# Recording the HGRN2 recurrence beside the next preparation, and stick-breaking attention as one pipeline over all query tiles

## The chip, the cores and the metric

The program runs on all 8 cores of one Trainium2 chip (two dies of four cores), two of the sixteen sequences on each core, the same program on every core. The metric is the device time in microseconds (us) of the slowest core. Such a program has two states: in some executions the cores of one die, or of both, show a lower granted TensorE clock and take some per cent longer. A run is called slow when one die is over 1% longer than the other at a lower clock, or when it is over 1.5% above the fastest run of the same kernel.

Engine names in the profile: PE is TensorE (PEld its weight loads), DVE is VectorE, ACT is ScalarE, POOL is GpSimd.

## The reference

Two layers of an encoder. Each layer is half a feed-forward step, a mixer with three branches (latent attention A, stick-breaking attention B, the gated recurrence HGRN2 C), a gated merge, another half feed-forward step and an added input embedding. The change touches branches B and C only:

```python
def stick_breaking_attention(q, k, v):            # 8 heads of 64, per block of queries
    z = einsum('bqhd,bkhd->bhqk', q, k) * scale
    mask = pos_k < pos_q
    log_beta = log_sigmoid(z)
    log_keep = where(mask, log_sigmoid(-z), 0.0)
    log_rest = cumsum(log_keep, reverse=True) - log_keep        # over the keys
    a = where(mask, exp(minimum(log_beta + log_rest, 0.0)), 0.0)
    return einsum('bhqk,bkhd->bqhd', a, v)

def hgrn2_recurrence(q_raw, f_raw, i_in, g_raw, lb, norm_w):    # 4 heads, chunks of 64
    ...                                                          # [cut: gates, cumulated logs]
    def step(state, xs):                                         # over the 32 chunks
        qd_n, kd_n, v_n, decay_n = xs
        o_n = einsum('bhck,bhkv->bhcv', qd_n, state)
        state = decay_n[..., None] * state + einsum('bhck,bhcv->bhkv', kd_n, v_n)
        return state, o_n
    ...                                                          # [cut: norm and output gate]
```

## The kernel before

The kernel records operations with the tiles that they read and write; a small layer turns these into semaphore waits, and each engine gets its operations in the order in which they were recorded. So the order of recording is the order of each engine's queue.

HGRN2, for each of the four heads: `prep` is a generator with 12 steps per tile of 512 tokens, and the four tiles take turns; then the recurrence runs alone.

```python
def prep(t, sl):
    mm(ps[b], [(whg[:, k, 128:256], uT[:, k, tok]) for k in range(8)])   # forget gate
    act(x1, ps[b], AF.Exp, scale=-1.0)
    yield
    mm(...); act(QF[:, tok], ps[b], AF.Silu); ts(x1, x1, 1.0, None, ALU.add)
    yield
    mm(...); act(GS[:, tok], ps[b], AF.Silu); reciprocal(x2, x1)          # VectorE
    yield
    ...          # [cut: V projection; Ln; scan; subtract; two Exp; three products; transposes]

interleave([prep(t0 + i, i) for i in range(min(NCHAIN, NT - t0))])        # four tiles
for t in range(NT):
    for j in range(4):
        mm1(ps[ba], KF[:, blk], QF[:, blk]); tt(Am, ps[ba], mhg_f, ALU.mult)   # mask product
        mm1(ps[bo], Vt[:, m, :], Am)
        for cch in range(2):                                              # two chunks
            mm1(ps[bo], Sbf[:, sl, :], QF[:, chunk])
            mm1(ps[bs_], KFt[pr, m, :], Vt[pr, m, :])
            stt(St, St, dec[:, c:c+1], ps[bs_], ALU.mult, ALU.add)
            ts(Sbf[:, 1 - sl, :], St, e1[:, c+1:c+2], None, ALU.mult)
    ...          # [cut: tail of a tile: Square, sum by matmul, Ln, Exp, two products]
```

Stick-breaking, for each of two groups of four heads: 16 query tiles (four heads, four tiles of 512), and for each a three-stage pipeline over blocks of 128 keys, which is emptied at the tile's end. A job is one block of keys. The first four jobs of a tile are its diagonal jobs, into whose blocks the mask cuts: they have 128, 256, 384 and 512 of the tile's queries. All later ones are full jobs of 512. In the comments below U is a triangle of ones, spb the masked logarithm and R its running sum over the keys already done.

```python
for hl in range(4):
    for tq in range(NT):
        for idx, kc in enumerate(range(nk - 1, -1, -1)):      # nk = 4, 8, 12, 16 jobs
            # stage 1: z = k.q ; Exp ; Ln(1 + .) ; mask ; R += (GpSimd and VectorE) ; Rb = bf16(R)
            # stage 2 of the job before: z again, + (-U).spb, + (-1).Rb, all into one bank ; Exp ; mask
            # stage 3 of the job before that: out += v.a
        ...      # [cut: the last two stages run out]
        cp(yB[...], ps[bo][0:64, :])                           # VectorE
```

The softmax here doesn't subtract the row's maximum and nothing guards it: scores larger than these inputs give would overflow.

Of the kernel before, what the change touches and what calls it, by code (L numbers as in the profile page):

```python
# [191 lines left out]
def build(nc, S, NSEQ, layers=(0, 1), phases=('ffa', 'mix', 'ffb', 'ple'), final_norm=True, dbg=None):  # L192
# [302 lines left out]
    def mixer(l, sq_i, branches):  # L495
# [152 lines left out]
        def branch_c():  # L648
# [29 lines left out]
            NCHAIN = min(4, NT)  # L678
# [7 lines left out]
            for h in range(4):  # L686
# [4 lines left out]
                def prep(t, sl):  # L691
# [6 lines left out]
                    b = bank()  # L698
# [3 lines left out]
                    b = bank()  # L702
# [4 lines left out]
                    b = bank()  # L707
# [4 lines left out]
                    b = bank()  # L712
# [31 lines left out]
                    b = bank()  # L744
# [10 lines left out]

                for t0 in range(0, NT, NCHAIN):
                    interleave([prep(t0 + i, i) for i in range(min(NCHAIN, NT - t0))])
                P.add('dve', lambda e: e.memset(St, 0.0), w=['St'])
                P.add('dve', lambda e: e.memset(Sbf[:, 0, :], 0.0), w=[('Sbf', 0)])
                ai = 0  # L760
                for t in range(NT):
                    tok = slice(t * 512, (t + 1) * 512)
                    bo = bank()
                    for j in range(4):
                        m = t * 4 + j
                        blk = slice(m * 128, (m + 1) * 128)
                        cols = slice(j * 128, (j + 1) * 128)
                        ba = bank_x(bo)
                        mm1(ps[ba][:, 0:128], KF[:, blk], QF[:, blk], True, True, r=[('KF', t), ('QF', t)], w=[PSK(ba)])
                        a_ = ai % 2  # L770
                        ai += 1
                        tt(Am[:, a_, :], ps[ba][:, 0:128], mhg_f, ALU.mult, r=[PSK(ba), 'cstf'], w=[('Am', a_)])
                        mm1(ps[bo][:, cols], Vt[:, m, :], Am[:, a_, :], True, False, r=[('Vt', t), ('Am', a_)], w=[PSK(bo)])
                        for cch in range(2):
                            c = 2 * m + cch
                            sl = c % 2
                            mm1(ps[bo][:, j * 128 + cch * 64:j * 128 + (cch + 1) * 64], Sbf[:, sl, :], QF[:, c * 64:(c + 1) * 64],
                                False, cch == 1, r=[('Sbf', sl), ('QF', t)], w=[PSK(bo)])
                            if c == NCH - 1:
                                continue  # L780
                            bs_ = bank_x(bo)
                            pr = slice(cch * 64, (cch + 1) * 64)
                            mm1(ps[bs_][:, 0:128], KFt[pr, m, :], Vt[pr, m, :], True, True, r=[('KFt', t), ('Vt', t)], w=[PSK(bs_)])
                            stt(St, St, dec[:, c:c + 1], ps[bs_][:, 0:128], ALU.mult, ALU.add, r=['St', PSK(bs_), ('dec', c // 8)], w=['St'])
                            ts(Sbf[:, 1 - sl, :], St, e1[:, c + 1:c + 2], None, ALU.mult, r=['St', ('e1', (c + 1) // 8)], w=[('Sbf', 1 - sl)])
                    sq = tmp['sq']
                    x1, x2 = X[0][0], X[0][1]
                    act(sq[:, 0, :], ps[bo][:, :], AF.Square, r=[PSK(bo)], w=[('sq', 0)])
                    bss = bank_x(bo)
                    mm1(ps[bss][:, :], ones_b, sq[:, 0, :], True, True, r=[('sq', 0), 'cstb'], w=[PSK(bss)])  # L790
                    act(x1, ps[bss][:, :], AF.Ln, r=[PSK(bss)], w=[('x', 0, 1)], scale=1.0 / 128, bias=epsc)
                    act(x1, x1, AF.Exp, r=[('x', 0, 1)], w=[('x', 0, 1)], scale=-0.5)
                    tt(x2, ps[bo][:, :], x1, ALU.mult, r=[PSK(bo), ('x', 0, 1)], w=[('x', 0, 2)])
                    stt(yC[:, h, tok], x2, nwcol(l, 37, h), GS[:, tok], ALU.mult, ALU.mult, r=[('x', 0, 2), ('GS', t), nwk], w=[('yT', 2)])
# [9 lines left out]
        def branch_b():  # L804
            for g in range(2):
# [35 lines left out]
                wi_ = 0  # L841
                for hl in range(4):
                    cc = hl // 2
                    pb = (hl % 2) * 64
                    hg = g * 4 + hl
                    for tq in range(NT):
                        qtok = slice(tq * 512, (tq + 1) * 512)
                        bo = bank()
                        nk = 4 * (tq + 1)
                        P.add('pool', lambda e: e.memset(R[:, 256:512], 0.0), w=[('R', 1)])  # L850
                        P.add('dve', lambda e: e.memset(R[:, 0:256], 0.0), w=[('R', 0)])
                        pend2 = None
                        pend3 = None
                        for idx, kc in enumerate(range(nk - 1, -1, -1)):
                            j = kc - 4 * tq
                            c0 = 128 * j if j > 0 else 0
                            cs = slice(c0, 512)
                            q = wi_ % 2
                            q3 = wi_ % 3
                            wi_ += 1  # L860
                            bz = bank_x(bo)
                            kap = kT[pb:pb + 64, cc, kc * 128:(kc + 1) * 128]
                            qap = qT[pb:pb + 64, cc, tq * 512 + c0:(tq + 1) * 512]
                            mm1(ps[bz][:, cs], kap, qap, True, True, r=[('kT', kc // 4), ('qT', tq)], w=[PSK(bz)])
                            act(e32[:, q, cs], ps[bz][:, cs], AF.Exp, r=[PSK(bz)], w=[('e32', q)])
                            act(spb[:, q3, cs], e32[:, q, cs], AF.Ln, r=[('e32', q)], w=[('spb', q3)], bias=onec)
                            if j >= 0:
                                tt(spb[:, q3, c0:c0 + 128], spb[:, q3, c0:c0 + 128], msb_b, ALU.mult, r=[('spb', q3), 'cstb'], w=[('spb', q3)])
                            if idx < nk - 1:
                                rs_ = idx % 4  # L870
                                jn = j - 1
                                c0n = 128 * jn if jn > 0 else 0
                                hi0 = max(c0, 256)
                                tt(R[:, hi0:512], R[:, hi0:512], spb[:, q3, hi0:512], ALU.add, r=[('R', 1), ('spb', q3)], w=[('R', 1)], eng='pool')
                                if c0 < 256:
                                    tt(R[:, c0:256], R[:, c0:256], spb[:, q3, c0:256], ALU.add, r=[('R', 0), ('spb', q3)], w=[('R', 0)])
                                cp(Rb[:, rs_, c0n:512], R[:, c0n:512], r=[('R', 0), ('R', 1)], w=[('Rb', rs_)])
                            p3 = pend3
                            pend3 = None
                            if pend2 is not None:  # L880
                                pend2()
                            if p3 is not None:
                                p3()

                            def stage3(idx=idx, kc=kc, cs=cs, q3=q3):
                                mm1(ps[bo][0:64, cs], vS[:, kc, hl * 64:(hl + 1) * 64], ab[:, q3, cs], idx == 0, idx == nk - 1,
                                    r=[('vS', kc // 4), ('ab', q3)], w=[PSK(bo)], skip=True)

                            def stage2(idx=idx, kc=kc, j=j, c0=c0, cs=cs, q3=q3, kap=kap, qap=qap, st3=stage3):
                                nonlocal pend3  # L890
                                bc = bank_x(bo)
                                rsl = (idx - 1) % 4

                                def fn(e):
                                    e.matmul(ps[bc][:, cs], kap, qap, start=True, stop=False)
                                    ins = e.matmul(ps[bc][:, cs], nuinc_b, spb[:, q3, cs], start=False, stop=(idx == 0))
                                    if idx > 0:
                                        ins = e.matmul(ps[bc][:, cs], nones_b, Rb[:, rsl, cs], start=False, stop=True)
                                    return ins
                                P.add('pe', fn, r=[('kT', kc // 4), ('qT', tq), ('spb', q3), 'cstb'] + ([('Rb', rsl)] if idx > 0 else []), w=[PSK(bc)])  # L900
                                act(ab[:, q3, cs], ps[bc][:, cs], AF.Exp, r=[PSK(bc)], w=[('ab', q3)])
                                if j >= 0:
                                    tt(ab[:, q3, c0:c0 + 128], ab[:, q3, c0:c0 + 128], msb_b, ALU.mult, r=[('ab', q3), 'cstb'], w=[('ab', q3)])
                                pend3 = st3
                            pend2 = stage2
                        if pend3 is not None:
                            p3 = pend3
                            pend3 = None
# [171 lines left out]
```

## Time and profile before

The six runs have a median of 14,892.7 us (14,829 to 15,087). The profiled run is a slow one.

I cut the trace at the first weight transfer of each stage (for the loops of B at the first clearing of the running sum R). The times are sums over four passes, mean of the eight cores:

| stage | us | mean TensorE clock, lowest to highest core |
|---|---|---|
| feed-forward, two halves | 4,123 | 0.92 to 0.97 |
| HGRN2 (C) | 1,940 | 0.62 to 0.63 |
| latent attention (A) | 1,987 | 0.82 to 0.84 |
| projections of B | 914 | 0.69 to 0.73 |
| the eight loops of B | 3,267 | 0.51 to 0.53 |
| merge and embedding | 2,464 | 0.90 to 0.95, 0.68 to 0.69 |

How to read the lines in this document: in a timeline a line is start, duration (us), engine, source line, operation, tiles, shapes; `x3` are three instructions that followed each other, and the bracket is the idle time of the engine before it and what ended it. `ps` are the banks that TensorE writes its sums to, `arena` the kernel's working memory, `cstb` and `cstf` constants such as the masks. In a table by stretch a line is the stretch and its length, then for each engine its busy time and number of instructions, then the granted TensorE clock and the DMA's share.

### The profile page before, as it was taken

What the parts mean: (1) busy time and instruction counts of PE and PEld (TensorE: products, weight loads), DVE (VectorE), ACT (ScalarE), POOL (GpSimd) and SP (SyncE); (2) the same over time, 40 slices, a digit from 0 to 9 for tenths busy, and PEclk for the clock granted to TensorE, in tenths of its full rate; (3) what the DMA queues carried; (4) which work ended last, traced back from release to release, by engine and by line L of the source; (5) the groups of instructions that cost most, each with busy time, mean ns of one, the idle gap of its engine ahead of it and who ended that gap; (6) DMA issues with size and microseconds to landing.
All of it is one profiled execution on the core that took longest, in us unless ns stands there. A gap on an engine that the chain in (4) does not pass through costs nothing.

```text
span 14948.8 us, 168234 instructions; the slowest of 8 cores (14713.2 to 14948.8 us)
## 1 busy us (share of the span) xinstructions
PE 11553.6 (77%) x44865; PEld 4260.9 (29%) x44865; DVE 5528.1 (37%) x10125; ACT 5259.7 (35%) x9306; POOL 2037.7 (14%) x2484
## 2 busy tenths in 40 slices
PE   6846778997964787899498467789989747778996
PEld 3322211343422211234233222113333322111342
DVE  2355433423244633331413553333222446333413
ACT  1224556312122555521211245562112225556212
POOL 0000122210100022211000001222101000123210
PEclk9868655998976855699677676557889868655997
DMA  4400000653621000266143000006545300000662
GB/s 73 54 6 8 5 5 1 59 69 47 71 25 11 5 1 5 25 65 70 56 60 41 10 4 5 5 1 56 59 54 63 40 7 4 5 5 9 65 71 47
DMA packets 1253066, 475.68 MB, mean 32 GB/s; under 512 B 838482, under 2 KB 1237428, under 8 KB 1251892
## 3 DMA queue, kind: packets, MB, share of 16 engines
q0 software_dynamic: 1233088, 420.02, 26.1%
q1 hardware_dynamic: 19060, 44.89, 0.9%
q8 instruction: 397, 6.50, 0.2%
q14 instruction: 521, 4.27, 0.1%
HBM read 868.01 MB, written 16.78 MB: 59 GB/s over the span
## 4 chain that ended last, share of the span: by engine, by line
PE 61%; DVE 13%; ACT 8%; DMA 8%; issue 8%; POOL 2%; DVEq 0%; ACTq 0%; POOLq 0%; SPq 0%
PE ps L117 60%; ACT arena L258 7%; DVE arena L269 6%; DVE arena L266 3%; DMA arena<-w_in 2%; POOL arena L266 2%; DVE arena L636 1%; DMA arena<-ffn_b_w_in 1%; DMA arena<-ffn_a_w_in 1%; DVE arena L274 1%; DMA arena<-w_out 1%; DMA arena<-p 1%; PE ps L121 1%; DVE arena L262 1%; DVEq L141 0%
## 5 line engine op out<-in xcount | busy, mean ns | idle before, releaser
L117 PE MATMUL ps<-arena 128*128 128x512 bf16 (+10 forms) x40304 | 9806.0, 392 | 2251.2 <-DVE arena L266 799.2
L117 PEld LDWEIGHTS ps<-arena 128*128 128x128 bf16 (+4 forms) x40304 | 3836.9, 103 | 8266.6 <-issue 5685.0
L258 ACT ACTIVATE arena<-ps 128x512 bf16<-128x512 f32 (+3 forms) x5584 | 3037.8, 552 | 6426.6 <-PE ps L117 6207.7
L117 PE MATMUL ps<-arena,cstb 128*128 128x512 bf16 (+3 forms) x3664 | 1726.9, 542 | 524.0 <-ACT arena L258 477.8
L266 DVE TENSOR_TENSOR arena<-arena,ps 128x512 bf16<-128x512 f32 (+1 forms) x1216 | 835.5, 688 | 2790.8 <-PE ps L117 2612.5
L258 ACT ACTIVATE arena<-hT 128x512 bf16<-128x512 f32 x1088 | 627.5, 623 | 1719.9 <-PE ps L117 999.0
L266 POOL TENSOR_TENSOR arena<-arena 128x256 f32<-128x256 f32 (+1 forms) x1152 | 934.9, 812 | 2157.2 <-DVE arena L266 1215.9
L269 DVE SCALAR_TENSOR_TENSOR arena<-hT,nw,arena 128x512 bf16<-128x512 f32 (+1 forms) x1088 | 817.5, 751 | 955.7 <-ACT arena L258 854.1
L266 DVE TENSOR_TENSOR arena<-arena 128x256 f32<-128x256 f32 (+4 forms) x1616 | 807.6, 514 | 631.2 <-ACT arena L258 559.4
L258 ACT ACTIVATE arena<-arena,onet 128x512 bf16<-128x512 f32 (+3 forms) x1280 | 843.8, 659 | 122.4 <-ACT arena L258 3.5
L274 DVE CAST arena<-arena 128x512 bf16<-128x512 f32 (+3 forms) x1162 | 478.7, 412 | 841.7 <-POOL arena L266 813.4
L117 PEld LDWEIGHTS ps<-arena,cstb 128*128 128x128 bf16 x3664 | 289.8, 107 | 1750.8 <-issue 1729.9
L246 POOL DMA_DIRECT2D arena<-w_in x292 | 257.9, 883 | 3133.8 <-PE ps L117 1238.3
L269 DVE SCALAR_TENSOR_TENSOR hT<-ps,hT 128x512 f32<-128x512 f32 x256 | 177.2, 692 | 1103.8 <-PE ps L117 1103.8
L274 DVE CAST arena<-ps 128x256 bf16<-128x256 f32 (+2 forms) x384 | 213.2, 555 | 956.8 <-PE ps L117 837.2
L266 DVE TENSOR_TENSOR arena<-arena,cstb 128x128 bf16<-128x128 bf16 x1536 | 329.2, 222 | 526.4 <-ACT arena L258 511.8
L636 DVE RECIPROCAL arena<-ps 64x512 f32<-64x512 f32 x128 | 429.9, 3359 | 49.4 <-PE ps L117 48.5
L246 POOL DMA_DIRECT2D arena<-ffn_a_w_in x176 | 154.1, 876 | 2077.5 <-PE ps L117 661.8
L121 PE MATMUL ps<-cstf,arena 128*128 128x128 f32 x640 | 148.8, 402 | 318.4 <-DMA arena<-x 143.3
L258 ACT ACT_TABLE_LOAD x116 | 148.8, 1283 | 530.5 <-PE ps L117 276.7
L246 POOL DMA_DIRECT2D arena<-ffn_b_w_in x176 | 153.9, 875 | 1208.3 <-PE ps L117 638.5
L258 ACT ACTIVATE arena<-arena 128x512 f32<-128x512 f32 (+1 forms) x616 | 276.9, 494 | 88.5 <-DVE arena L266 60.9
(75 smaller groups left out, 2635.6 us busy)
## 6 DMA issues: line engine op xcount, KB each, us to landing
arena<-ffn_a_w_in POOLq DMA_DIRECT2D x176, 512.0 KB, 6.0
arena<-ffn_b_w_in POOLq DMA_DIRECT2D x176, 512.0 KB, 6.0
arena<-w_in POOLq DMA_DIRECT2D x256, 256.0 KB, 4.4
arena<-ffn_a_w_out POOLq DMA_DIRECT2D x64, 704.0 KB, 8.2
arena<-ffn_b_w_out POOLq DMA_DIRECT2D x64, 704.0 KB, 8.3
arena<-x SPq DMA_DIRECT2D x32, 512.0 KB
arena<-w_out POOLq DMA_DIRECT2D x64, 256.0 KB, 4.7
out<-arena SPq DMA_DIRECT2D x32, 512.0 KB
```

What stands on the lines that cost most here:

```text
L117: return nc.tensor.matmul(*a, **k)
L121: return nc.tensor.transpose(*a, **k)
L246: return P.add(eng, lambda e: e.dma_start(out=out, in_=in_), r=r, w=w, dma=True)
L258: return P.add('act', lambda e: e.activation(out, in_, func, bias=bias, scale=scale), r=r, w=w)
L262: return P.add(eng, lambda e: e.tensor_scalar(out, in0, s1, None, op0), r=r, w=w)
L266: return P.add(eng, lambda e: e.tensor_tensor(out, in0, in1, op), r=r, w=w)
L269: return P.add('dve', lambda e: e.scalar_tensor_tensor(out, in0, sc, in1, op0, op1), r=r, w=w)
L274: return P.add(eng, lambda e: e.tensor_copy(out, in_), r=r, w=w)
L636: P.add('dve', lambda e, bo=bo, rsl=rsl: e.reciprocal(rec[0:64, rsl, :], ps[bo][64:128, :]), r=[PSK(bo)], w=[('rec', rsl)])
```

## The change

Intent: run the recurrence of one half of a head while the next half is prepared, and let the stick-breaking pipeline run through the boundaries of the tiles. Core of the diff:

```diff
-            NCHAIN = min(4, NT)
+            NCHAIN = max(1, min(2, NT // 2)) if NT > 1 else 1
 ...                                  # banks 0-5 for HGRN2, 6 and 7 for its outputs
-                for t0 in range(0, NT, NCHAIN):
-                    interleave([prep(t0 + i, i) for i in range(min(NCHAIN, NT - t0))])
-                ...                  # recurrence over all tiles, alone
+                def rec(tiles, h=h):
+                    for t in tiles:
+                        ...          # the same recurrence, a yield after each chunk, three in the tail
+                g1 = [prep(t, i) for i, t in enumerate(first)]
+                if pending_rec is not None:
+                    g1.append(pending_rec)
+                interleave(g1)
+                g2 = [prep(t, i) for i, t in enumerate(second)]
+                g2.append(rec(first))
+                interleave(g2)
+                pending_rec = rec(second) if second else None
 ...
-                for hl in range(4):
-                    for tq in range(NT):
-                        ...          # pipeline per tile, with its own drain
+                jobs = [...]         # all (hl, tq, idx, kc): 160 in a loop
+                for n in range(NJB + 2):
+                    if n < NJB:
+                        st[n][0]()
+                    if 0 <= n - 1 < NJB:
+                        st[n - 1][1]()
+                    if 0 <= n - 2 < NJB:
+                        st[n - 2][2]()
 ...
-                        cp(yB[...], ps[bo][0:64, :], ...)
+                            cp(yB[...], ps[bo][0:64, :], ..., eng='act')
```

## The prediction

> **What bounds the kernel now.** I read the list of cores first. The profile fell in the slow state: 14,948.8 us on core 5, die 1 about 1% behind die 0. The six timed runs have a median of 14,892.7 us. Then came the page's busy line, and the busy time by stretch of core 5 for the first of four passes (two sequences times two layers), cut where the tell-tale instructions stand (the 512-wide reciprocals for HGRN2, the memsets of the running sum R for stick-breaking).
>
> ```profile
> PE 11553.6 (77%) x44865; PEld 4260.9 (29%) x44865; DVE 5528.1 (37%) x10125; ACT 5259.7 (35%) x9306; POOL 2037.7 (14%) x2484
> core 5: us, PE busy (x) PEld busy (x) DVE busy (x) ACT busy (x) POOL busy (x), PEclk, DMA share, GB/s
> 684.00:726.00 42.00, 25.65 (x210) 15.46 (x211) 32.14 (x40) 19.01 (x41) 3.50 (x4) 0.78 0.25 22
> 726.00:789.00 63.00, 22.15 (x108) 9.82 (x107) 27.95 (x87) 8.04 (x13) 0.00 (x0) 0.50 0.03 3
> 1734.00:2140.00 406.00, 347.89 (x784) 64.89 (x784) 141.02 (x416) 268.76 (x481) 122.01 (x160) 0.52 0.00 1
> ```
>
> The average of 77% TensorE mixes stages. The two that the change touches are HGRN2 (644 to 1,122 us, 478 us a pass) and the stick-breaking loop (1,734 to 2,140 and 2,253 to 2,659: two loops of 406 us a pass). Both run mostly at half the TensorE clock (0.50, 0.52), while the FFN stretches beside them have 0.96 to 0.97. The loop of stick-breaking is 8 x 406 = 3,248 us of the kernel, HGRN2 4 x 478 = 1,912 us.
>
> Next the timeline inside the loop. In its steady part a job (one block of 128 keys) takes 2.49 us, from one Exp of z to the next:
>
> ```profile
> 1910.52 0.60 ACT L258 ACTIVATE arena<-ps 128x512 f32<-128x512 f32 x1 [0.50 <-PE ps L117]
> 1910.78 1.04 PE L117 MATMUL ps<-arena,cstb 128*128 128x512 bf16 x2
> 1911.75 1.59 PE L117 MATMUL ps<-arena 128*64 128x512 bf16 x3
> 1913.01 0.60 ACT L258 ACTIVATE arena<-ps 128x512 f32<-128x512 f32 x1 [0.50 <-PE ps L117]
> ```
>
> The five 512-wide matmuls of a job follow without a gap, 0.5 us apiece, so TensorE at half clock is the bound; ScalarE waits 0.5 us a job for it. At the end of each of the 16 query tiles of a loop the pipeline drains:
>
> ```profile
> 1892.55 0.60 ACT L258 ACTIVATE arena<-ps 128x512 f32<-128x512 f32 x1 [0.50 <-PE ps L117]
> 1896.89 0.60 ACT L258 ACTIVATE arena<-ps 128x512 bf16<-128x512 f32 x1 [2.35 <-PE ps L117]
> 1898.55 0.28 ACT L258 ACTIVATE arena<-ps 128x128 f32<-128x128 f32 x1 [1.06 <-PE ps L117]
> 1905.18 0.60 ACT L258 ACTIVATE arena<-ps 128x512 f32<-128x512 f32 x1 [0.17 <-PE ps L117]
> ```
>
> From the last full Exp (1892.55) to the first one of the next tile (1898.55) 6.0 us pass, not 2.49, and ScalarE stands idle for 2.35 and 1.06 us of it.
>
> In HGRN2 a head takes 110.5 us (first reciprocals at 688.5, next head's at 799.0): preparation of all four tiles, 47.7 us (PE start 788.7 to 836.4), then the recurrence, some 62.5 us, of which each pair of chunks is 3.15 us of ping-pong:
>
> ```profile
> 749.68 0.28 DVE L266 TENSOR_TENSOR arena<-ps,cstf 128x128 bf16<-128x128 f32 x1
> 750.11 0.53 PE L117 MATMUL ps<-arena 128*128 128x128 bf16 x3 [0.97 <-DVE arena L266]
> 750.75 0.35 DVE L269 SCALAR_TENSOR_TENSOR arena<-arena,ps 128x128 f32<-128x128 f32 x1 [0.79 <-PE ps L117]
> 751.21 0.29 DVE L262 TENSOR_SCALAR arena<-arena 128x128 bf16<-128x128 f32 x1
> 751.64 0.65 PE L117 MATMUL ps<-arena 128*128 128x64 bf16 x3 [1.00 <-DVE arena L262]
> 752.18 0.35 DVE L269 SCALAR_TENSOR_TENSOR arena<-arena,ps 128x128 f32<-128x128 f32 x1 [0.69 <-PE ps L117]
> 799.00 12.98 DVE L710 RECIPROCAL arena<-arena 128x512 f32<-128x512 f32 x4
> ```
>
> VectorE waits 0.7 to 0.8 us for TensorE in each chunk and TensorE 1.0 us for VectorE. The last line matters below: a reciprocal holds VectorE for 3.3 us.
>
> **What the Trainium skill says.** "TensorE: Matmul & The Clock Gate", Part 1, has a clock gate with two states, 4/8 and 8/8, driven by activity over windows of about 3.4 us. The trace agrees in the states (clock records of 0.5 and 1.0, in multiples of 3.41 us) but not with "busy means warm": the loop is at half clock in 388 of 406 us with TensorE hardly pausing. "PSUM — Partial Sum Buffer", Engine vs sequencer instructions: the queues of ScalarE and VectorE are strict FIFO. The trace agrees as far as it goes (VectorE's order is the program's); this decides what the HGRN2 overlap can give. "ScalarE: Activation LUTs", What ACT_TABLE_LOAD costs: about 1,283 ns a load; the page's row has 1283 ns for 116 loads.
>
> **The change, stick-breaking.** Nothing is added or removed but the tile boundary: the 160 jobs of a loop become one three-stage pipeline, and the copy of a finished tile moves from VectorE (0.68 us) to ScalarE (about 0.6 us, which has 0.5 us a job to spare). Tiles with 4, 8, 12, 16 jobs take 11.0, 20.5, 30.5, 40.5 us (differences of the finishing copies 1744.9 to 1847.4). With 0, 4, 8, 12 full jobs at 2.49 us, that leaves 10.6 us a tile (11.0 for the shortest) for its four diagonal jobs together with drain and fill. In a closed pipeline the four cost TensorE's time alone: matmul pitch 0.20, 0.29, 0.39, 0.50 us at widths 128, 256, 384, 512 from the timeline, four matmuls for the first job and five for each other: 0.8 + 1.45 + 1.95 + 2.5 = 6.7 us. I add 0.4 us, because the chain z, Exp, Ln, mask and the copy of the tile on ScalarE reach the short jobs late: 7.1 us. Saved: 3.5 us a boundary; 15 boundaries in each of 8 loops, 120 in all: **420 us**.
>
> A second effect is the clock. In the few stretches of a loop at full clock (core 5: 99 us of 3,220 in all; the cores have 71 to 168) a job takes 1.79 us instead of 2.49, bound by ScalarE. [...] Without drains the mean fill rises from about 0.70 to 0.80. I guess full clock in 250 us instead of 100, worth 150 x (2.49/1.79 - 1) = **60 us**. This is my least certain number.
>
> **The change, HGRN2.** The head is split into two halves of two tiles; each half's preparation is recorded in turns with one chunk of the recurrence of the half before. Work is the same, but for 32 more table loads (four a head, not two), beside other work. Both engines take their queues in order, so I walked one half through, with the durations above (12 rounds of preparation, 22 of recurrence). Rounds 1 to 4 (four 1.73 us projections for two tiles, 13.8 us, plus 2 us cold start): the recurrence adds a wait for the mask product in rounds 1 and 3, and in round 3 the mask product stands behind two reciprocals (6.5 us), so TensorE idles some 4 us: 23 us instead of 16. Rounds 5 to 12: on VectorE scans, subtractions and products (8 us for two tiles) plus five chunks and the tail of a tile, each chunk still with its own 0.8 us round trip where the mask product is in it: to about 42 us. Then seven chunks alone, 11 us: the half takes 54 us before TensorE can go on. Alone, the preparation of two tiles is 27.5 us and the recurrence 31.5, so only some 5 us of 59 are hidden. A pass: first half 31 (it stands behind the norm on VectorE), seven halves of 54, last recurrence 31.5: 440 us against 447.5 now. If the 4 us hole of round 3 drops the clock, the V projections cost 2 to 3 us more a half, 18 a pass. I take **+5 us a pass, +20 us in all**: nothing gained.
>
> Sum: -420 - 60 + 20 = -460 us; I shade it to -440: **14,450 us**, 3.0% less.
>
> **The rivals.** (a) The HGRN2 overlap works as named: if the recurrence went wholly beside the preparation, VectorE's 64 us a head (33 of preparation, 31 of recurrence from the rows) would be the bound in place of 110.5; with some fill left, 40 us a head, 16 heads, 640 us would go beside the 420: 13,850 us. For it: VectorE is busy only 28 of 63 us in the recurrence. Against it: in-order queues and 22 rounds against 12. (b) The in-order blocking is worse than I walked it (cold projections, transposes behind a waiting chunk): +20 us a pass, 80 in all; the whole saves 380 us or less, 14,530. (c) The diagonal jobs are bound by latency, not by TensorE: 8.5 instead of 7.1 us, saving 250 us: 14,650, within 2%. For it: short jobs have 1 us of TensorE work against a chain of some 1.5 us from z to the masked Ln. (d) The clock turns up for half of the loop's time: 300 us more gone, 14,150.
>
> **Range and chances.** The boundary can be worth 250 to 450 us, the clock 0 to 250, HGRN2 -80 to +100. Together I expect 14,300 to 14,640 in 8 of 10 cases. Faster by 2% means under 14,595: 0.84; within 2% 0.15; slower 0.01.
>
> **What would show it.** Finishing copies of tiles now on ScalarE, about 37, 27, 17 and 7 us apart for 16, 12, 8 and 4 jobs; a loop of 350 us; jobs in the middle still at 2.49 us and clock near 0.55. HGRN2 at 470 to 490 us a pass with halves of 54 us, holes of 4 us in TensorE under each pair of reciprocals, 148 table loads. FFN, merge and latent attention as before. The prediction is wrong if halves of HGRN2 take 40 us, if the loop's clock goes well above 0.6, or if a loop stays over 380 us.

## The result, and the profile after

The changed kernel takes 14,502.2 us (median of 20 runs, 14,321.7 to 14,765.4) against 14,921.6 us (40 runs). The ratio is 0.9725, with a 95% interval of 0.9686 to 0.9763: faster by 2.75%. A ratio here is the mean time of one kernel's fast runs over that of the other's of the same rounds, so it is not quite the ratio of the medians.

By stage (as above, us; the two profiles are both slow):

| stage | before | after | difference |
|---|---|---|---|
| HGRN2 | 1,940 | 1,876 | -64 |
| eight loops of B | 3,267 | 2,937 | -330 |
| latent attention | 1,987 | 1,982 | -5 |
| projections of B | 914 | 915 | +1 |
| feed-forward, merge, embedding | 6,588 | 6,627 | +39 |

The last row is the same code, at a lower clock in the first feed-forward of this one profile (0.89 to 0.95 against 0.92 to 0.97), and is not an effect of the change. The two parts touched give 394 us, and the fast runs' ratio agrees with it (0.0275 x 14,900 = 410, by the interval 353 to 468).

The stretches of the changed kernel on core 5: one half of a head in HGRN2, and the two loops of the first pass.

```profile
807.10:859.72 52.62, 27.54 (x171) 14.72 (x170) 30.21 (x63) 16.27 (x30) 0.00 (x0) 0.69 0.00 0
1768.50:2138.60 370.10, 348.53 (x784) 64.83 (x784) 131.94 (x400) 276.72 (x497) 122.11 (x160) 0.52 0.00 1
2252.80:2616.90 364.10, 338.47 (x786) 64.81 (x784) 132.50 (x400) 275.17 (x497) 120.97 (x160) 0.54 0.00 1
```

The loops took 406 us before. In the first loop TensorE's busy time is as it was (348 us), so it is the idle time that went: 58 us before, 22 now (in the second 60 and 26). The finishing copies of the tiles, on ScalarE now, show it tile by tile (timeline, ScalarE alone):

```profile
1797.55 0.57 ACT L273 CAST arena<-ps 64x512 bf16<-64x512 f32 x1
1824.33 0.57 ACT L273 CAST arena<-ps 64x512 bf16<-64x512 f32 x1
1861.99 0.57 ACT L273 CAST arena<-ps 64x512 bf16<-64x512 f32 x1
1870.24 0.58 ACT L273 CAST arena<-ps 64x512 bf16<-64x512 f32 x1
1888.27 0.58 ACT L273 CAST arena<-ps 64x512 bf16<-64x512 f32 x1
```

Tiles of 4 and 8 jobs now take 8.25 and 18.0 us; in the later tiles of the loop, outside the stretches at full clock, those of 12 and 16 take 28.06 and 37.96. Before it was 11.0, 20.5, 30.4 and 40.4. Full jobs still take 2.50 us here (2.49 in the median of all cores), with ScalarE waiting 0.51 us for TensorE in each (timeline, ScalarE; the two other functions of the job left out):

```profile
1905.69 0.60 ACT L258 ACTIVATE arena<-ps 128x512 f32<-128x512 f32 x1 [0.51 <-PE ps L117]
...
1908.19 0.60 ACT L258 ACTIVATE arena<-ps 128x512 f32<-128x512 f32 x1 [0.51 <-PE ps L117]
```

So the diagonal part of a tile is 8.1 us (28.06 - 8 x 2.49), where the prediction has 7.1. Where the rest of it stands is seen at one boundary (timeline, one tile boundary of the first loop, at about 1,888 us; lines of other jobs left out):

```profile
1887.99 0.26 ACT L258 ACTIVATE arena<-ps 128x128 bf16<-128x128 f32 x1
1888.18 0.23 DVE L266 TENSOR_TENSOR arena<-arena,cstb 128x128 bf16<-128x128 bf16 x1 [1.31 <-ACT arena L258]
1888.27 0.58 ACT L273 CAST arena<-ps 64x512 bf16<-64x512 f32 x1
1888.55 0.67 POOL L266 TENSOR_TENSOR arena<-arena 128x256 f32<-128x256 f32 x1 [2.07 <-DVE arena L266]
...
1889.33 0.36 DVE L274 CAST arena<-arena 128x384 bf16<-128x384 f32 x1 [0.92 <-POOL arena L266]
...
1889.60 0.22 DVE L266 TENSOR_TENSOR arena<-arena,cstb 128x128 bf16<-128x128 bf16 x1
1889.97 1.14 PE L117 MATMUL ps<-arena 128*64 128x128 bf16 x3 [0.50 <-DVE arena L266]
```

The weights of the first diagonal job leave ScalarE at 1888.25. Their mask product on VectorE runs at 1889.60, because in VectorE's queue it stands behind the cast of R, which waits for GpSimd's sum. TensorE's value matmul waits for it.

In HGRN2 the half has the hole that the prediction describes (timeline of the half that starts at 807.1):

```profile
818.15 6.56 DVE L720 RECIPROCAL arena<-arena 128x512 f32<-128x512 f32 x2
...
824.62 0.23 DVE L266 TENSOR_TENSOR arena<-ps,cstf 128x128 bf16<-128x128 f32 x1
825.00 5.77 PE L117 MATMUL ps<-arena 128*128 128x128 bf16 x70 [4.00 <-DVE arena L266]
```

The mask product of the recurrence stands behind two reciprocals, and TensorE is idle for 4.00 us. The profile page counts 148 loads of ScalarE's function tables, as foretold:

```profile
L258 ACT ACT_TABLE_LOAD x148 | 189.9, 1283 | 595.6 <-PE ps L117 324.1
```

### The profile page after: what moved, and what is told of

The parts are those of the page before. It is cut to its first block, busy times and chain, and to the rows that moved or that the text cites. A ratio compares the mean times of both kernels' runs of the same rounds, so it can differ in the third digit from the quotient of the medians.

```text
span 14549.3 us, 168524 instructions; the slowest of 8 cores (14407.1 to 14549.3 us)
## 1 busy us (share of the span) xinstructions
PE 11514.1 (79%) x44865; PEld 4299.4 (30%) x44865; DVE 5449.2 (37%) x9997; ACT 5342.7 (37%) x9466; POOL 2037.1 (14%) x2484
## 4 chain that ended last, share of the span: by engine, by line
PE 62%; DVE 13%; DMA 9%; issue 7%; ACT 6%; POOL 1%; DVEq 0%; ACTq 0%; POOLq 0%; SPq 0%
PE ps L117 62%; DVE arena L269 6%; ACT arena L258 6%; DVE arena L266 2%; DMA arena<-w_in 2%; DMA arena<-ffn_b_w_in 2%; DVE arena L636 1%; DVE arena L720 1%; DMA arena<-ffn_a_w_in 1%; POOL arena L266 1%; PE ps L121 1%; DMA arena<-w_out 1%; DMA arena<-p 1%; DVE arena L262 1%; DMA arena<-ffn_b_w_out 1%
## 5 line engine op out<-in xcount | busy, mean ns | idle before, releaser
L117 PEld LDWEIGHTS ps<-arena 128*128 128x128 bf16 (+4 forms) x40304 | 3879.2, 105 | 7953.4 <-issue 5388.8
L258 ACT ACTIVATE arena<-ps 128x512 bf16<-128x512 f32 (+2 forms) x5584 | 3025.6, 551 | 5629.2 <-PE ps L117 5416.2
L273 ACT CAST arena<-ps 64x512 bf16<-64x512 f32 (+1 forms) x384 | 222.3, 579 | 531.7 <-PE ps L117 523.9
L269 DVE SCALAR_TENSOR_TENSOR arena<-arena,ps 128x128 f32<-128x128 f32 x496 | 171.4, 346 | 485.2 <-PE ps L117 485.2
```

What stands on the lines that cost most here:

```text
L117: return nc.tensor.matmul(*a, **k)
L258: return P.add('act', lambda e: e.activation(out, in_, func, bias=bias, scale=scale), r=r, w=w)
L269: return P.add('dve', lambda e: e.scalar_tensor_tensor(out, in0, sc, in1, op0, op1), r=r, w=w)
L273: return P.add('act', lambda e: e.copy(out, in_), r=r, w=w)
```

## The experiments

They ran later than the 20 runs above, in four groups (e1 to e4; e5 to e8; e9 and e10; e11 and e12), each on another chip and beside the kernel before. That kernel then took 15,232 to 15,535 us (medians), and most runs were slow. In the longer profiles it is the feed-forward that is longer, at a lower clock (4,264 us at 0.87 to 0.95 in e1, against 4,123 before). So none of them has a clear verdict on the whole time: the record has a ratio of fast runs for e4 alone, 0.974 (0.955 to 0.993), unclear. I judge by the two stages concerned, taken from each run's profile in the same way. These hardly depend on the state: in six profiles with the loops of the change (the change itself twice, e1, e6, e9, e10) the eight loops took 2,930 to 2,939 us, and in seven with its HGRN2 that stage took 1,874 to 1,888 us. All twelve runs were correct.

**e1: the flat pipeline alone; e2: the HGRN2 overlap alone.** The edit is one of the two halves of the diff above.

> Only the flat stick-breaking pipeline, HGRN2 as before. Theory (the saving is drain and fill at 120 tile boundaries, measured 2.5 to 2.9 us each in the profile of the change): the eight loops together 2,937 us against 3,267 before, HGRN2 unchanged at 1,940 us, ratio to before 0.978 (0.976 to 0.980). Rival (the two parts depend on each other, or part of the loops' gain comes from the clock left behind by the other part): loops above 2,980 us, ratio over 0.983.

> Only the HGRN2 overlap, stick-breaking as before. Theory (in-order queues let the overlap hide only some 5 us of each half): HGRN2 1,876 us over four passes against 1,940 before, loops unchanged at 3,267 us, ratio 0.9957 (0.993 to 0.998), inside 2%. Rival (overlap is worth what the title of the change hopes, and the full change hides it elsewhere): ratio under 0.985.

Measured: e1 loops 2,935 us, HGRN2 1,944 us; e2 loops 3,262 us, HGRN2 1,881 us. The two parts are independent, and their stage times add up. On the whole time the medians are 14,837 and 15,094 us against 15,260 before; there were not enough fast runs for an interval (e1: its one fast run, 14,531 us, is under both fast runs of before, 15,104 and 15,140; e2: its one, 15,026, is too, by 0.5%). So five sixths of the gain is the tile boundaries, and the HGRN2 overlap is worth some 60 us.

**e3: the finishing copy back on VectorE.**

```diff
-                            cp(yB[...], ps[bo][0:64, :], ..., eng='act')
+                            cp(yB[...], ps[bo][0:64, :], ...)
```

> The change, but with the finishing copy of a tile on VectorE again. Theory (at the boundary the copy on ScalarE, 0.58 us, stands before the Exp of the third diagonal job and delays it): the diagonal part of a tile falls from 8.1 to about 7.6 us, eight loops about 2,880 us against 2,937, ratio to the change 0.996. Rival (VectorE's queue is the one that blocks at the boundary, since the mask products wait there behind casts that wait for GpSimd, so a copy of 0.68 us there costs as much or more): loops 2,937 us or longer.

Measured: loops 2,946 us against 2,937; tiles at 8.2, 18.1, 28.1 and 37.9 us. Nothing is gained: my theory of the copy fell. The rival's number came true, but its reason is not shown: the copy may cost as much in the one queue as in the other, or nothing in either.

**e7: the third stage one job later; e4: a longer pipeline altogether.**

```diff
 # e7                                          # e4
-ab = AR.alloc([3, 512], BF)                   -ab, spb = 3 slots each ; Rb 4
+ab = AR.alloc([4, 512], BF)                   +ab, spb = 4 slots each ; Rb 6
-    st[n - 2][2]()                            -    st[n - 1][1]() ; st[n - 2][2]()
+    st[n - 3][2]()                            +    st[n - 2][1]() ; st[n - 4][2]()
```

> The change with the third stage alone one job later (three jobs behind the first, one more slot for the weights). Theory (the largest wait at a boundary is that of the value matmul for the mask product of the weights, which stands on VectorE behind a cast that waits for GpSimd): the diagonal part of a tile falls from 8.1 to about 7.4 us, loops to about 2,850 us. Rival (the waits are those of the second stage for the masked logarithm, which only the second stage's own delay removes): loops within 25 us of 2,937.

> The change with a longer pipeline: the second stage two jobs behind the first (not one), the third four behind (not two), with one more slot for the two bf16 tiles and two more for the bf16 copies of R. Theory (the 8.1 us that the diagonal jobs still take are 6.7 us of TensorE at half clock and 1.4 us of waiting for masks and copies that stand in order behind others): the diagonal part falls to 6.7 to 7.0 us, eight loops about 2,937 - 128 x 1.2 + 8 x 5 for the longer fill = 2,820 us, ratio to the change 0.992. Rival (short matmuls cost TensorE more than I took, so the 8.1 us are its own time): loops stay within 20 us of 2,937, or get longer by the fill.

Measured: e7 loops 2,857 us, with tiles of 7.8, 17.3, 27.3 and 37.2 us, so a diagonal part of 7.4 us: the wait for the mask product of the weights is 0.7 us of it, as expected. e4 loops 2,693 us, more than was expected. Its finishing copies (timeline, ScalarE alone):

```profile
1724.77 0.57 ACT L273 CAST arena<-ps 64x512 bf16<-64x512 f32 x1
1741.46 0.57 ACT L273 CAST arena<-ps 64x512 bf16<-64x512 f32 x1
1768.16 0.57 ACT L273 CAST arena<-ps 64x512 bf16<-64x512 f32 x1
1804.53 0.57 ACT L273 CAST arena<-ps 64x512 bf16<-64x512 f32 x1
1811.35 0.58 ACT L273 CAST arena<-ps 64x512 bf16<-64x512 f32 x1
```

Tiles of 8, 12 and 4 jobs: 16.7, 26.7 and 6.8 us. The diagonal part is 6.7 to 6.8 us (26.70 - 8 x 2.49), which is TensorE's own time as worked out in the prediction. So 1.35 us of the change's 8.1 us is waiting for masks and sums, in both stages, and none of it is a cost of short matmuls. That is 128 x 1.35 = 173 us. The rest of the 244 us is mostly clock: by the clock records full clock in 308 us of a core's loop time (mean of eight) against 173 in the change, worth by estimate (2.49/1.79 - 1) x 135 = 53 us. These two make 226 of 244.

**e5: z multiplied once.** The sums are accumulated onto the bank that already holds z, so a job has four matmuls in place of five and takes one bank in place of two; nothing else changes.

```diff
-                        bc = zbank()
+                        bc = zbk[0]                    # the bank of stage 1's z
-                            e.matmul(ps[bc][:, cs], kap, qap, start=True, stop=False)
                             ins = e.matmul(ps[bc][:, cs], nuinc_b, spb[:, q3, cs], start=False, ...)
```

> The change, but z is multiplied once: the two sums are accumulated onto the bank that still holds it, so a job has four matmuls, not five, with ScalarE's and VectorE's work as it was. Theory (inside a tile the loop is bound by TensorE at half clock, 0.5 us a matmul): a full job falls from 2.49 to 2.0 us, 96 full jobs in each of 8 loops, -384 us, the diagonal jobs up to -100 us, less 50 us for fewer stretches at full clock: eight loops 2,530 us (2,450 to 2,600) against 2,937. Rival (a round of waits through ScalarE, VectorE and GpSimd sets the 2.49 us and TensorE only happens to be full): loops over 2,850 us.

Measured: loops 2,560 us, in the range. The steady part of a loop (timeline):

```profile
1834.66 1.04 PE L117 MATMUL ps<-arena,cstb 128*128 128x512 bf16 x2
1834.83 0.60 ACT L258 ACTIVATE arena<-ps 128x512 f32<-128x512 f32 x1 [0.17 <-PE ps L117]
1835.63 1.17 PE L117 MATMUL ps<-arena 128*64 128x512 bf16 x2
1836.89 0.60 ACT L258 ACTIVATE arena<-ps 128x512 f32<-128x512 f32 x1 [0.17 <-PE ps L117]
```

A job takes 2.06 us, and ScalarE's wait for TensorE fell from 0.5 to 0.17 us. The bound inside a tile was TensorE at half clock, as read from the profile before. It took 0.43 us off a job and not 0.5, because 0.5 is a mean: in the records of the change at half clock, 512-wide matmuls start 0.40 us after one that uses as many rows and columns of the array, and 0.56 to 0.57 us after one that uses other ones; the z that went was one of the first kind. I had expected less time at full clock; there was more (543 us a core).

**e6: the recurrence's step first in each round.**

```diff
-                    g1.append(pending_rec)
+                    g1.insert(0, pending_rec)
-                g2.append(rec(first))
+                g2.insert(0, rec(first))
```

> The change, but in each round of HGRN2 the recurrence's step is recorded before the two preparations, not after. Theory (the mask product of the third round stands behind two reciprocals on VectorE, and TensorE idles 4 us in each half): that hole goes, a half falls from 52.5 to about 49 us, HGRN2 over four passes from 1,876 to about 1,780 us. Rival (the time of a half is the sum of VectorE's chain and moves to another wait): HGRN2 above 1,850 us.

Measured: HGRN2 1,882 us; halves of mostly 54 to 55 us on the profiled core, where the change has 52 to 54. The theory fell. The hole under the reciprocals did go, and holes as large opened elsewhere (timeline of one half and the beginning of the next):

```profile
800.39 9.31 PE L117 MATMUL ps<-arena 128*128 128x128 bf16 x86 [0.55 <-DVE arena L266]
801.58 6.56 DVE L720 RECIPROCAL arena<-arena 128x512 f32<-128x512 f32 x2
...
827.26 0.53 PE L117 MATMUL ps<-arena 128*128 128x128 bf16 x3 [5.61 <-DVE arena L266]
...
843.58 11.22 PE L117 MATMUL ps<-arena 128*128 128x128 bf16 x38 [3.59 <-DVE arena L266]
```

TensorE works through the reciprocals, but waits 5.61 us for a mask product behind the products of the preparation, and 3.59 us at the head of the next half, where its first step now waits for the tail of the tile before.

**e9: the sigmoid on ScalarE, without a reciprocal.** If VectorE's chain as a whole sets a half, then only taking work out of it helps.

```diff
                     act(x1, ps[b][:, :], AF.Exp, ..., scale=-1.0)
+                    act(x1, x1, AF.Ln, ..., bias=onec)
+                    act(x2, x1, AF.Exp, ..., scale=-1.0)
-                    ts(x1, x1, 1.0, None, ALU.add, ...)
-                    P.add('dve', lambda e: e.reciprocal(x2, x1), ...)
```

> The change, but in HGRN2 the sigmoid is made on ScalarE as Exp(-Ln(1 + Exp(-x))), all in the first round where that table set is loaded; VectorE loses the addition and the reciprocal (3.65 us a tile), ScalarE gains two functions of 0.6 us. Theory (VectorE's chain, with each chunk's round trip, sets a half; the two reciprocals are 6.6 us of it): a half falls from 52.5 to 46 to 48 us, HGRN2 over four passes from 1,876 to 1,700 to 1,750 us. Rival (the hole under the reciprocals is free time, as it moved elsewhere when the recurrence was put first): HGRN2 above 1,830 us.

Measured: HGRN2 1,731 us; halves of 47 to 48 us in 174 of 192 cases (eight cores, without each pass's first), 50 to 51 in the others. A half of it by engine, core 1 (a line of the table by stretch):

```profile
784.45:832.00 47.55, 26.29 (x172) 13.67 (x171) 23.20 (x59) 19.04 (x35) 0.00 (x0) 0.72 0.00 1
```

VectorE has 23.2 us of work against 30.2 in the change, and the half is 5.1 us shorter; ScalarE's 2.8 us more cost nothing. The 4 us hole under the reciprocals went too (TensorE waits 0.55 us there), so this run alone does not part the two; but e6, which took the hole away and left VectorE's work, gained nothing. Together they hold the theory: the time goes when VectorE's work goes, not when TensorE's hole is moved.

**e10: two steps of the recurrence in each round.** A wrapper takes two steps of `rec` for one of each `prep`.

> The change, but the recurrence takes two steps in each round of HGRN2, so that it ends with the preparation (11 rounds, not 22). Theory (each chunk costs its own round trip wherever it stands, and only the wait of every other chunk can hide): a half gets 0 to 3 us shorter, HGRN2 1,800 to 1,880 us. Rival (the 10 rounds of recurrence alone at the end of a half are what keeps the overlap from paying): a half falls to some 42 us, HGRN2 under 1,650 us.

Measured: HGRN2 1,906 us, 18 to 32 us longer than the seven profiles named above. My own range missed by 26 us: I had not expected a loss. The rival falls clearly: it is not the ten rounds of recurrence alone at the end of a half that keep the overlap from paying. That fits the theory that a chunk costs its round trip wherever it stands; what makes the stage longer is not shown.

**e8 and e11: together; e12: the change again.** e8 is e4, e5 and e6 together; e11 is e4, e5 and e9.

> The change with the longer pipeline, the single z and the recurrence first, together. If the three add up: full jobs at 2.0 us, diagonal part about 5.5 us, eight loops 2,300 to 2,400 us; HGRN2 about 1,780 us; ratio to before 0.925 to 0.935. If ScalarE becomes the bound (1.92 us a job from its three functions back to back): loops not under 2,300 us. If the effects overlap: loops over 2,450 us.

> The change with the longer pipeline, the single z and the sigmoid on ScalarE; the recurrence stands last in its round as in the change. If the parts add up: loops 2,231 us as in the run of the first two together (with the recurrence first), HGRN2 1,731 us as with the sigmoid alone; 1,245 us less than before, ratio 0.917 (0.90 to 0.93). If a lower clock in the dense stages takes part back: those two stages as said, ratio over 0.93.

> The change itself on the same chip, for the comparison with the best version: ratio 0.9725 (0.965 to 0.98), loops 2,937 us, HGRN2 1,876 us.

| | loops of B, us | HGRN2, us | runs (n), us | fast run |
|---|---|---|---|---|
| e8 | 2,232 | 1,884 | 13,925 to 14,434 (9) | none |
| e11 | 2,225 | 1,758 | 13,897 to 14,397 (7) | 13,922.9 |
| e12, the change | 2,936 | 1,884 | 14,444 to 15,279 (6) | 14,443.8 |
| before, beside e11 and e12 | | | 14,885 to 15,833 (11) | 14,884.9 |

In e8 HGRN2 missed the 1,780 us expected, as e6 had. The effects in the loops of B more than add up (2,937 to 2,225): with four matmuls and the longer pipeline the median distance of two full jobs on ScalarE is 1.79 us even at half clock (in tiles wholly at half clock it is still 2.08, from 22.21 us for 12 jobs and 13.87 for 8). HGRN2 in e11 is 1,732 and 1,736 us on the two cores whose clock was best and up to 1,767 on the others. The best version beats both kernels: all seven of its runs lie under all six of the change, and its one fast run is 0.964 of the change's one and 0.935 of the one of before. Ratios of single runs have no interval, and 0.935 is a smaller gain than the 0.917 expected. By the stages the 1,224 us are there (3,267 + 1,940 - 2,225 - 1,758), and the fastest core of any run shows nearly as much: 13,440 us against 14,635 before and 14,265 for the change (825 us, where the stages of e12 and e11 differ by 837). But the slowest core of a run also carries the clock of its feed-forward stages, 0.84 to 0.93 in this profile. Whether that clock is lower because of the change or by the chip's state in those minutes, these runs do not tell.

## Why the prediction was right

The total and the direction held: 14,502 us against 14,450 foretold. The terms were less good, and it is in part luck that they made up for each other:

| term | foretold, us | measured, us |
|---|---|---|
| tile boundaries | -420 | about -306, the rest of the loops' -330 |
| clock in the loops | -60 | about -24, an estimate |
| HGRN2 | +20 | -64 |
| sum | -460 (stated as -440) | -394 |

- **Bound of the loop: right.** Full jobs stayed at 2.49 us, and e5, which took one of five matmuls away, brought a job to 2.06 us. "0.5 us apiece" holds only as a mean (see e5).
- **Boundaries: mechanism right, one term mis-sized.** The prediction put it as "I add 0.4 us, because the chain z, Exp, Ln, mask and the copy of the tile on ScalarE reach the short jobs late". It measured 1.35 us (8.1 against e4's 6.75). TensorE's own 6.7 us was right. The reason named was only in part the right one: e3 shows that nothing is won by taking the copy off ScalarE, and e7 that about half of it is the wait for the mask product of the weights, behind the cast of R in VectorE's queue; the rest went when e4 delayed the second stage too. Rival (c), diagonal jobs bound by latency, was thus true in kind, at 8.1 and not 8.5 us.
- **Clock: direction right, size too high.** I guessed full clock in 250 us in place of 100. Over the eight cores the means are 112 us before and 173 after; (2.49/1.79 - 1) x 61 = 24 us. The guess leaned on a count of how often a well filled window is followed by full clock; it does not come out of the traces. Counted again over all loops before, in windows of 3.41 us at half clock (fill is streamed columns over 4,096): full clock or 13/16 followed 37 of 2,915 windows filled to 0.83 or more, 39 of 2,402 at 0.6 to 0.83 and none of 736 at 0.5 to 0.6. The mean fill did rise, from 0.70 to 0.78.
- **HGRN2: the walk was good, the step after it wrong.** Halves take 53.0 us in the mean of the profiled core, against 54 foretold, with the hole of 4 us where it was put; the walk's own result was 7 us a pass gained. The first half took 27.5 us, not 31. The step that failed is "I take +5 us a pass": 12 us of it were for a clock drop under the hole. The trace has that drop (half clock from 824.6 to 828.0), and it falls within halves that still take 52 to 54 us. Over the whole stage the mean clock rose, from 0.62 to 0.66. Rival (b) fell with it.
- **Rival (a), overlap that works as named: rightly put low.** e2 shows 60 us of the 640 that it would have brought; e6 and e10 show that neither order nor the number of rounds brings the rest, and e9 that 7.0 us less work for VectorE in a half bring 5.1 us.
- **Rival (d)** did not come: the loops' clock is 0.52 to 0.55.

## What to carry to other kernels

Where engines take their queues in the order of recording, interleaving two chains hides only what neither needs the same engine for; walk one round through with measured durations before expecting an overlap, and take work off the engine both chains share rather than moving the hole. In a software pipeline, count what each boundary costs as measured period minus full jobs, and then compare it with the bound engine's own time: the difference is what a stage of delay more can still win. When an engine is full at half clock, a recomputed product that was free at full clock (here a job took 1.79 us there, set by ScalarE) is the first thing to remove.

## What the Trainium skill lacked or had wrong

- "TensorE: Matmul & The Clock Gate", Part 1, explains the clock by busyness over windows of about 3.4 us, with the warm state after a busy window. Here the loops of B stay at half clock while five 512-wide matmuls a job follow without a gap in the records: only 112 us of 3,267 us a core were at full clock before, and 308 us of 2,693 in e4, where TensorE waits least with five matmuls a job. The stretches above half clock were 13.65 us long in 76 of 140 cases before. What else decides, these runs do not tell.
- The same page, Back-to-back issue gap, gives N/1.2 ns at half clock for isolated matmuls, 427 ns for N = 512. In the loops of the change two starts are 0.40 us apart where both matmuls use as many rows and columns (6,592 cases of 128x128 after 128x128), 0.56 to 0.57 where they do not, and 2.49/5 = 0.50 us in the mean.
- The same page's 13/16 clock agrees: records of 0.8125 appear in all profiles. How the clock of the dense stages varies from run to run at the same code (0.83 to 0.97 over these profiles, core by core) is on no page.
- "PSUM — Partial Sum Buffer" has a synchronised read in the middle of an accumulation group as allowed. e5 agrees: accumulating onto a bank that ScalarE had read in between gave correct results.
- No page that I read gives VectorE's reciprocal a duration: 3.3 us for 128x512 f32, against 0.42 to 0.75 us for other operations of that shape here, and 1.2 us for a scan.
